# A hybrid decoder trunk on one core: the instruction order of every engine computed with another machine model of the library

## The chip, the cores and the metric

The kernel runs on one core of one Trainium2 chip. The metric is device time in microseconds of one launch; lower is better. The time before is 1925.44 us, the median of three runs.

## The reference

Two layers over a residual stream of 1024 tokens by 1024 features, all in float32. Each layer normalises the stream, multiplies it with one wide input matrix, feeds slices of the product to four mixers, gates each mixer with its own SiLU path, multiplies the joined result with an output matrix, normalises again and adds it to the stream; then a gated embedding is added.

```python
for i in range(DEPTH):
    h = rms_norm(x, g_pre[i])
    proj = h @ w_in[i]
    (q, k_cmp, v_cmp, k_sel, v_sel, k_win, v_win, nsa_g, z_a,
     u, v, z_b, glu_a, glu_b, z_c, rw, z_d) = jnp.split(proj, split_at, axis=-1)
    y_a = nsa_attention(...)
    y_b = spatial_gating(u, v, ...)
    y_c = conv_module(glu_a, glu_b, ...)
    y_d = rwkv7_time_mix(token_shift(rw, ...), ...)
    mix = concat([y_a * silu(z_a), y_b * silu(z_b), y_c * silu(z_c), y_d * silu(z_d)])
    x = x + rms_norm(mix @ w_out[i], g_post[i])
    x = x + sigmoid(x @ ple_gate[i]) * (p[i] @ ple_proj[i])
```

The attention has a compressed, a selected and a windowed branch. The RWKV mixer is a recurrence over time, which the kernel computes in chunks of 64 tokens.

## The kernel before, in words

The work is cut into two layers and, in each, two halves of 512 tokens. For each of these four parts a string of letters in ORDER gives the steps in the order in which the program writes them: H the norm, F the RWKV projections, R the small triangular solves of RWKV, r its serial chunk steps, N and A the attention, G, T and C the convolution, s the spatial gating, a to d the gate projections, O, x and g the output projection, residual and embedding gate.

Dense products are made at full precision by splitting each float32 operand into a high and a low part: `mm3` (L163 to L165) issues three matmuls of 128x128 weights by 128x512 activations for each product. The weights come in granules of 128x512: `split_w` (L149 to L159) loads one by SyncE's queue (L154), ScalarE casts its high part (L157), GpSimd subtracts to get the low part (L158). Each of the three tiles has a ring of three buffers, and these four instructions carry a priority 4000 places ahead of where they are written:

```python
with self.tc.high_priority(offset=4000):
    st = self.t([128, 512], "ws")
    for ap, w in src:
        nc.sync.dma_start(ap(st), w)
    hi = self.t([128, 512], "wh", dt=F32R)
    lo = self.t([128, 512], "wl", dt=F32R)
    nc.scalar.copy(hi[:, :cols], st[:, :cols])
    nc.gpsimd.tensor_sub(lo[:, :cols], st[:, :cols], hi[:, :cols].bitcast(F32))
```

PSUM has two banks for dense products ("mm"), two for attention scores ("s"), and one each for RWKV ("rp", "c1"), transposes ("pt") and attention sums ("pv").

Nothing in the kernel writes out an engine's queue. The program is traced in the order of ORDER and handed to the library's tile scheduler when the TileContext closes. The scheduler is a list scheduler: it steps a machine model through time; whenever the model says that an engine can take an instruction, the scheduler gives it, of those whose inputs and buffers the model says are ready, the one with the highest priority (the place in the program, moved ahead by `high_priority`). The sequence in which an engine was given its instructions becomes its queue, and on the chip each queue runs in that order: an instruction whose input is late holds all that stand behind it on its engine. SyncE's queue of DMA issues is made in the same way. So the model's durations decide the order and nothing else: the tiles, the buffers, the instructions and their dependencies come from the program.

Places that the prediction speaks of:

- `compress_out` (L846 on): on TensorE L856 (first product of the compression, on weights that a DMA brings) and L862, on ScalarE L866, on VectorE L867 (SiLU), on TensorE L870 (second product).
- `rwkv_solve` (L444 on): on VectorE a serial loop of 15 and one of 16 rounds; the second is L500 (multiply) and L502 (reduce).
- `rwkv_tri` L533 and L539, `rwkv_pair` L377, `a_block` L438 and L441.
- `rwkv_step` (L558 on), eight times in a half: TensorE L578 and L582, ScalarE L585, TensorE L589, VectorE and ScalarE L591 and L592, TensorE L602, VectorE L611, TensorE L616. Each group of matmuls waits for the other engine's result just before it, and L582 of the next step waits for L611.
- `rwkv_norm` (L620 on): GpSimd L630 (a power, 16 elements per partition), for which VectorE's L632 waits. `rstd` L243 is the same operation with 1 to 4 elements; L265 on TensorE waits for it.
- `branch` (L975 on): scores L994 and L995, exponent L1024 on ScalarE, L1029 on VectorE scales the probabilities; `attn_tile` L957 transposes them on TensorE, L960 and L961 split them, L966 and L967 multiply with the values.
- `conv_taps` L683: 240 multiply-adds of 128x512 on VectorE.

## Time and profile before

| | us |
|---|---|
| median of 3 runs | 1925.44 |
| the three runs | 1922.86, 1925.44, 1941.99 |
| the profiled execution's own time | 1919.29 |
| its span, first to last instruction | 1917.6 |
| TensorE busy in the span | 1725.0 |
| VectorE, ScalarE, GpSimd busy | 1383.7, 813.6, 612.2 |

The rows of the profile come from the one profiled execution. An engine's idle time before an instruction is put down to the engine or DMA whose result came last ("<-"). The end of a matmul is modelled, so its duration is longer than the time until the next one can start: the distance between starts is the better measure of what a matmul costs in a dense run.

### The profile page before, as it was taken

The page shows a single profiled execution, that of the slowest core. Times are in us where ns is not written, and L with a number is a line of the kernel's source. Part 1 is how long each engine was busy: PE and PEld are TensorE (multiplying, and loading weights), DVE is VectorE, ACT ScalarE, POOL GpSimd, SP SyncE. Part 2 cuts the span into 40 slices and gives each one's busy share as a digit, 9 for nine tenths or more (in the row PEclk, how much of TensorE's full clock was granted, in tenths as well). Part 3 has the DMA queues.
Part 4 walks back from the last instruction along what each step waited for, and adds up shares of the span by engine and source line. Part 5 has one row for each costly group of instructions (what it writes and reads, how often), then busy time and mean ns, then how long its engine had stood idle before and what let it go on. Part 6 is the DMA issues. An engine that isn't in the chain of part 4 may idle for free. (4 is left out here: it accounts for less than half of the span.)

```text
span 1917.6 us, 27663 instructions
## 1 busy us (share of the span) xinstructions
PE 1725.0 (90%) x9444; PEld 1296.7 (68%) x9444; DVE 1383.7 (72%) x3361; ACT 813.6 (42%) x1805; POOL 612.2 (32%) x487
## 2 busy tenths in 40 slices
PE   5797998899799999899888999989988989989998
PEld 4565776566577667666666767766666767766777
DVE  4449787887888865977578881869778789476554
ACT  4332234544223455655232343545432445545543
POOL 2223343122342333322233346322232232422253
PEclk8898999999899999999998999999998999979999
DMA  6435233123432231532253233542253223223444
GB/s 208 90 87 107 71 97 84 45 57 64 114 81 78 67 99 63 169 106 55 60 123 78 69 115 117 166 121 56 62 113 79 53 57 115 66 72 109 139 139 152
DMA packets 326148, 182.23 MB, mean 95 GB/s; under 512 B 88300, under 2 KB 299248, under 8 KB 326008
## 3 DMA queue, kind: packets, MB, share of 16 engines
q1 hardware_dynamic: 326008, 180.47, 34.7%
q8 instruction: 74, 1.21, 0.3%
q14 instruction: 66, 0.54, 0.1%
HBM read 149.98 MB, written 30.44 MB: 94 GB/s over the span
## 5 line engine op out<-in xcount | busy, mean ns | idle before, releaser
L158 POOL TENSOR_TENSOR wl<-ws,wh 128x512 fp32r<-128x512 f32 (+2 forms) x388 | 521.6, 1346 | 1160.7 <-ACT wh L157 1021.0
L163 PE MATMUL mm<-aT,wh 128*128 128x512 f32 (+1 forms) x1304 | 538.2, 416 | 16.6 <-ACT t L667 7.4
L164 PE MATMUL mm<-aT,wh 128*128 128x512 f32 (+1 forms) x1304 | 536.3, 411 | 8.3 <-DVE aT L252 8.0
L165 PE MATMUL mm<-aT,wl 128*128 128x512 f32 (+1 forms) x1304 | 535.4, 411 | 0.4 <-POOL wl L158 0.4
L157 ACT CAST wh<-ws 128x512 fp32r<-128x512 f32 (+2 forms) x388 | 236.9, 611 | 454.3 <-PE mm L164 229.4
L163 PEld LDWEIGHTS mm<-aT,wh 128*128 128x128 f32 (+1 forms) x1304 | 251.0, 193 | 71.0 <-ACT t L667 7.9
L164 PEld LDWEIGHTS mm<-aT,wh 128*128 128x128 f32 (+1 forms) x1304 | 252.1, 193 | 60.5 <-DVE aT L252 15.2
L165 PEld LDWEIGHTS mm<-aT,wl 128*128 128x128 f32 (+1 forms) x1304 | 251.6, 193 | 48.2 <-issue 2.6
L683 DVE SCALAR_TENSOR_TENSOR cv<-cv,cw,cv 128x512 f32<-128x512 f32 x240 | 213.4, 905 | 3.2
L961 DVE TENSOR_TENSOR pt<-pt,pt 128x512 fp32r<-128x512 f32 (+1 forms) x152 | 93.7, 617 | 122.2 <-ACT pt L960 120.9
L1024 ACT ACTIVATE r<-s,sma 128x512 f32<-128x512 f32 (+3 forms) x192 | 106.2, 555 | 111.2 <-DVE sma L1022 76.3
L960 ACT CAST pt<-pt 128x512 fp32r<-128x512 f32 (+1 forms) x152 | 80.3, 528 | 112.7 <-PE pt L957 112.3
L957 PE MATMUL pt<-cst,r 128*128 128x128 f32 x528 | 98.4, 282 | 21.9 <-DVE r L1029 16.9
L957 PEld LDWEIGHTS pt<-cst,r 128*128 128x128 f32 x528 | 64.2, 143 | 50.8 <-DVE r L1029 26.3
L967 PE MATMUL pv<-pt,vs 128*128 128x256 f32 x264 | 79.0, 317 | 11.8 <-DVE pt L961 10.2
L966 PE MATMUL pv<-pt,vs 128*128 128x256 f32 x264 | 84.7, 321 | 2.4 <-ACT pt L960 2.1
L994 PE MATMUL s<-kv,qs 128*128 128x512 f32 (+2 forms) x192 | 75.6, 394 | 4.9 <-ACT r L1024 4.7
L1029 DVE TENSOR_SCALAR r<-r,sma 128x640 f32<-128x640 f32 (+7 forms) x128 | 76.1, 595 | 0.8
L967 PEld LDWEIGHTS pv<-pt,vs 128*128 128x128 f32 x264 | 50.6, 192 | 35.1 <-DVE pt L961 28.3
L966 PEld LDWEIGHTS pv<-pt,vs 128*128 128x128 f32 x264 | 50.6, 192 | 32.3 <-ACT pt L960 26.7
L995 PE MATMUL s<-kv,qs 128*128 128x512 f32 (+2 forms) x192 | 65.7, 345 | 0.0
L994 PEld LDWEIGHTS s<-kv,qs 128*128 128x128 f32 x192 | 37.1, 193 | 34.5 <-ACT r L1024 27.2
(333 smaller groups left out, 2904.1 us busy)
## 6 DMA issues: line engine op xcount, KB each, us to landing
ws<-in_w_in_dram SPq DMA_DIRECT2D x232, 256.0 KB, 2.9
ws<-in_ple_gate_dram SPq DMA_DIRECT2D x64, 256.0 KB, 2.8
ws<-in_w_out_dram SPq DMA_DIRECT2D x60, 256.0 KB, 2.8
ped<-ot SPq DMA_DIRECT2D x32, 256.0 KB, 3.4
ld<-in_nsa_w_dram SPq DMA_DIRECT2D x32, 256.0 KB, 3.5
ld<-ped SPq DMA_DIRECT2D x32, 256.0 KB, 3.5
mixd<-y SPq DMA_DIRECT2D x30, 256.0 KB, 2.0
ld<-mixd SPq DMA_DIRECT2D x30, 256.0 KB, 3.0
```

Source lines behind the costliest of these rows:

```text
L157: nc.scalar.copy(hi[:, :cols], st[:, :cols])
L158: nc.gpsimd.tensor_sub(lo[:, :cols], st[:, :cols], hi[:, :cols].bitcast(F32))
L163: nc.tensor.matmul(out, lh, rh, start=first, stop=False, skip_group_check=shared)
L164: nc.tensor.matmul(out, lh, rl, start=False, stop=False, skip_group_check=shared)
L165: nc.tensor.matmul(out, ll, rh, start=False, stop=last, skip_group_check=shared)
L683: nc.vector.scalar_tensor_tensor(ac, xg[j][:, k:k + TH], cw[:, j * 31 + k:j * 31 + k + 1], ac, op0=OP.mult, op1=OP.add)
L957: nc.tensor.transpose(pt[:, o:o + 128], P[e][:, (b + x - b0) * 128:(b + x - b0) * 128 + 128], self.ident)
L961: nc.vector.tensor_sub(Tl[:, :n], pt[:, :n], Th[:, :n].bitcast(F32))
L966: nc.tensor.matmul(acc, vs, Th[:, x * 256:x * 256 + 256], start=False, stop=False)
L967: nc.tensor.matmul(acc, vs, Tl[:, x * 256:x * 256 + 256], start=False, stop=last)
L994: nc.tensor.matmul(p[:, :n], w.QS[hd][:, qs], w.KH[br, hh][:, c0 * 128:c1 * 128], start=True, stop=False)
L1024: nc.scalar.activation(P[:, o:o + wd], p[:, c:c + wd], AF.Exp, bias=ng[:, 0:1], accum_out=den[:, x:x + 1])
```

## The change

One argument of the TileContext. The scheduler now steps the library's timeline machine instead of its core machine. The timeline machine walks each instruction through its sequencer, its engine's queue, the engine and its semaphores as separate resources; the core machine is the library's default model. The traced program, its 27663 instructions, their tiles, priorities and buffer rings stay as they are; the order of each engine's queue is what comes out differently.

```diff
-    with _tile.TileContext(nc) as tc:
+    with _tile.TileContext(nc, schedule_with_timeline_sim=True) as tc:
         tile_trunk_kernel(tc, aps)
```

## Rows read from the trace of the kernel before

**Rows 1.** The page, first lines: span, and TensorE's busy time, share, instructions.

```profile
span 1917.6 us, 27663 instructions
...
PE 1725.0 (90%) x9444; PEld 1296.7 (68%) x9444; DVE 1383.7 (72%) x3361; ACT 813.6 (42%) x1805; POOL 612.2 (32%) x487
```

**Rows 2.** The waits of TensorE: total us, times, longest us.

```profile
PE pt L870 <- DVE cth L867: 17.4, 3, 8.2
PE pt L957 <- DVE r L1029: 16.9, 23, 3.5
PE pt L856 <- DMA ld<-in_nsa_w_dram: 10.9, 9, 3.3
PE rp L377 <- ACT t L374: 10.3, 1, 10.3
PE pv L967 <- DVE pt L961: 10.2, 17, 3.8
PE mm L163 <- ACT t L1054: 10.2, 1, 10.2
PE rp L533 <- DMA x<-Xd: 9.0, 4, 5.3
PE mm L163 <- ACT t L667: 7.4, 2, 6.9
PE mm L163 <- ACT ot L1063: 7.2, 3, 6.5
PE c L441 <- DVE q L459: 7.0, 4, 2.3
PE mm L265 <- POOL smc L243: 6.3, 6, 1.4
```

**Rows 3.** The timeline of TensorE in layers 0 and 1: start, duration, what [idle before].

```profile
177.88 0.43 PE L870 MATMUL pt<-cth,w 128*64 128x31 f32 x4 [8.22 <-DVE cth L867]
...
1442.17 0.43 PE L870 MATMUL pt<-cth,w 128*64 128x32 f32 x4 [8.23 <-DVE cth L867]
1442.53 0.80 PE L165 MATMUL mm<-aT,wl 128*128 128x512 f32 x1
```

**Rows 4.** The timeline of VectorE just before the second of these.

```profile
1441.25 0.61 DVE L500 TENSOR_TENSOR q<-l,q 128x248 f32<-128x248 f32 x1
1441.89 0.22 DVE L867 SCALAR_TENSOR_TENSOR cth<-cth,pt 128x64 f32<-128x64 f32 x1
```

**Rows 5.** The timeline of TensorE, 641 to 647 us.

```profile
646.03 0.30 PE L957 MATMUL pt<-cst,r 128*128 128x128 f32 x1 [3.53 <-DVE r L1029]
646.09 0.48 PE L163 MATMUL mm<-aT,wh 128*128 128x512 f32 x1
```

**Rows 6.** The timeline of VectorE at the same place.

```profile
643.62 1.25 DVE L632 TENSOR_SCALAR yt<-yt,bmv,bmr 128x64 f32<-128x64 f32 x1 [2.90 <-POOL bmr L630]
...
645.34 0.54 DVE L1029 TENSOR_SCALAR r<-r,sma 128x640 f32<-128x640 f32 x1
```

**Rows 7.** Groups of instructions: count, busy us, mean ns, idle before us.

```profile
L630 POOL TENSOR_TENSOR bmr<-bmr,mhalf 128x16 f32<-128x16 f32 x4 | 12.2, 3054 | 1.1 <-DVE bmr L629 1.0
```

**Rows 8.** Stretches: length, busy time of the five engines, granted clock, DMA share, GB/s.

```profile
1441.00:1448.00 7.00, 5.83 (x20) 4.25 (x21) 5.48 (x13) 2.13 (x7) 0.24 (x1) 0.61 0.18 16
1152.00:1176.00 24.00, 23.79 (x105) 19.32 (x105) 1.20 (x2) 9.86 (x18) 14.39 (x13) 1.00 0.45 138
```

**Rows 9.** The timeline of TensorE: the same group in two successive RWKV steps.

```profile
612.51 0.82 PE L616 MATMUL c<-l,at 64*64 64x64 f32 x8
...
620.75 0.82 PE L616 MATMUL c<-l,at 64*64 64x64 f32 x8
```

**Rows 10.** The timeline of TensorE in a dense stretch, three matmuls apart.

```profile
1160.08 0.39 PE L163 MATMUL mm<-aT,wh 128*128 128x512 f32 x1
...
1160.76 0.39 PE L163 MATMUL mm<-aT,wh 128*128 128x512 f32 x1
```

**Rows 11.** One line, the convolution taps: ns min/median/max, first and last start.

```profile
L683 DVE SCALAR_TENSOR_TENSOR cv<-cv,cw,cv x240: 681/750/1859, 179.7 to 1612.2; 128x512 f32<-128x512 f32 x120
```

## The prediction

> **What bounds the kernel now.** I read the page first: TensorE is busy 1725.0 us of a span of 1917.6 [rows 1], so it is idle 1917.6 - 1725.0 = 192.6 us. The second engine, VectorE, is busy 1383.7 us and stays under the span by 534 us. TensorE sets the time, and since the change leaves its instructions alone, what an order can give is a part of the 192.6 us and of what the clock takes. The second view is TensorE's waits [rows 2]: the reader is to see that the long entries are not dense matmuls (L163 to L165) that starve for weights. GpSimd's low part of the weights is not among the long entries. They are small matmuls of the chains (L870, L957, L967, L533, L441) that stand at the head of the queue while their input is late. The third view is the timeline at two of these places. At 1442.17 us L870 had waited 8.23 us for VectorE's L867 [rows 3], and the matmul right behind it is L165, the third of a dense product whose first two were already done: its operands were there, and it could have run in the wait, with what follows it. VectorE came late because L867 stands behind the rounds of the solve, the last but a reduce of which began at 1441.25 [rows 4]. The same wait occurs in layer 0, 8.22 us long [rows 3], and the two make most of the 17.4 us of rows 2; so it is not chance: the machine that made the order had VectorE through the solve some 8 us earlier, against TensorE, than the chip has it. The second place is of the same kind: TensorE's L957 waits 3.53 us with a dense L163 behind it [rows 5]; its input L1029 stands on VectorE behind L632, which itself waited 2.90 us for GpSimd's L630 [rows 6], a power that takes 3.05 us four times [rows 7]. A queue that knew of these 3 us would have put L1029 and what it needs ahead of L632.
>
> **What the change does to these terms.** It removes and adds no instruction, so every duration stays; what moves is the place of instructions in five queues, SyncE's DMA issues included. I take the waits of rows 2 in three classes.
>
> Waits for a result of VectorE or GpSimd whose lateness the order misjudged, with dense work behind: L870 17.4, L957 16.9, L265 6.3, together 40.6 us. The cover is there: a dense product of three matmuls starts every 0.68 us [rows 10], so 8 us of wait is 36 of them, as many as three granules hold. The ends are 0 (the new order misjudges the same) and 40.6; I take 35, since two of the three lines show their cause in the rows and the cause is one of durations, which is what a machine model has to offer.
>
> Waits on hops and DMA landings: L856 10.9, L967 10.2, L533 9.0, L441 7.0, together 37.1 us. Here the issue and the use are both in the order's hands, but the chains in question are tight, with 17 waits of L967 that average 0.6 us. Ends 0 and 37.1; I take a quarter, 9, the value nearest to the many short waits.
>
> Waits that have no other work behind them, or are of dense matmuls themselves: on L374 10.3 (L377, at the start, before other work exists), on L1054 10.2, on L667 7.4, on L1063 7.2, together 35.1 us. They wait for operands or for a PSUM bank to be emptied. Ends: 35.1 saved to 35.1 lost, as an order can relieve or deepen them; I take 0.
>
> [...]
>
> New waits: no trace shows them. The smallest long row of rows 2 that is a chain wait is L441 with 7.0, the largest L870 with 17.4; I take 7 as the price of one new place, and keep 0 and 52 (three times 17.4) as ends.
>
> VectorE's and ScalarE's own waits are not priced, as only what reaches TensorE counts; SyncE's issues are in the class of the DMA waits. Moving the weight splits is costed at nothing because the ring of three granules hides them now, as TensorE's long waits show none on them [rows 2]; if that cover went, a granule late is 4 x 0.68 = 2.7 us.
>
> One thing no order can settle in advance: a tap of the convolution takes 681 to 1859 ns for the same shape [rows 11], so either machine's clock for VectorE drifts from the chip's in these stretches. [...]
>
> Sum: 35 + 9 + 5 - 7 = 42 us. The profiled execution took 1919.3 us, so 1877. The median of the runs stands 6.1 us above it, so I forecast 1883 us for the median, 2.2% less than 1925.4.
>
> **The rivals.** First, slower: the timeline machine has a queue in front of each engine as a resource of its own, and so an instruction may be given to an engine long before it starts. If the scheduler fills such a queue with ready dense matmuls, a chain matmul that becomes ready a moment later goes behind them, for good. The place is the RWKV step: L616 follows L616 after 620.75 - 612.51 = 8.24 us [rows 9], with three groups of matmuls in turn (L589, L602, L616 with the next L582) that each answer to another engine. One granule more ahead of each is 4 x 0.68 = 2.72 us [rows 10], three times in a step and 32 steps: 261 us of longer chains, 65 in each of the four parts. TensorE does other work meanwhile, as long as there is any: the rival decides where the attention, gates and projections that the buffers admit are used up before the chain ends. If a quarter stays uncovered it costs 65 us: 1925 + 65 = 1990. For it: TensorE has gaps in the serial stretches already, so the remaining work there is thin. Against it: a queue with more dense work between hops also has fewer waits of the class of 37.1.
>
> Second, no change: the gaps are set by buffers. In the trace the cases for it are L667 and L1063, 14.6 us of PSUM banks; the chain waits of 77.7 speak against it. If filling a wait early only makes the two dense banks or the three granules run out sooner, the gain of 42 comes back as waits of the third class: 1920 to 1930. [...]
>
> Third, it does not do what it says: priorities and dependencies fix the queues so tightly that the order hardly differs; 1925.
>
> **How the numbers follow.** The forecast 0.50, the slower rival 0.30, the buffers 0.14, no new order 0.06. About 1% is what a measurement of this kernel can tell from no change, that is 1906 to 1945. So faster 0.50, same 0.20, slower 0.30. The forecast's own range is 1842 (all of 40.6 and 37.1 and the clock, 83 us) to 1906. The whole range begins lower, at 1815: a third of the 79.8 us of idle that the listed rows leave (192.6 - 77.7 - 35.1) may go with the rest, 83 + 27 = 110. It ends at 1990, the price of the slower rival; a tenth lies above it, where more than a quarter of the chain is bare, and less below the lower end.
>
> **What would show it.** Right: the two 8.2 us waits before L870 gone, the 17.4 under 4; L957's 16.9 under 8; TensorE idle at 150 us or less with the same busy time; L632 on VectorE no longer with L1029 behind it in its wait. The slower rival: the distance of L616 to L616 well over 8.24 us, and TensorE's idle time in stretches with little dense work. The buffers: the idle time moves from chain lines to L163 waiting for ScalarE or VectorE. The forecast is wrong if TensorE's idle time grows, or if its idle time falls and the busy time grows as much, by more switches between small and dense matmuls or a lower clock.

## The result, and the profile after

The kernel after takes 2106.53 us in the median (2097.53 to 2117.51), the kernel before 1933.72 us beside it: a ratio of 1.092 [1.088, 1.097]. The change makes it 9% slower; the forecast was 2.2% faster. The profiled execution of after took 2117.51 us; it stands 198 us above that of before. The medians differ by 173 us: after's profiled execution is the slowest of its four, and before's is faster than the four that the ratio goes by.

The page of after: span, busy times, then four of the rows with 40 equal slices of the span.

```profile
span 2115.8 us, 27584 instructions
...
PE 1866.7 (88%) x9444; PEld 1445.2 (68%) x9444; DVE 1364.4 (64%) x3361; ACT 810.1 (38%) x1805; POOL 632.4 (30%) x487
...
PE   4899789889969999899979999899997999989878
...
PEclk8999775579979887999969897999997958779879
DMA  7344320012434200442332331352433301045133
```

The same two last rows of before:

```profile
PEclk8898999999899999999998999999998999979999
DMA  6435233123432231532253233542253223223444
```

TensorE has the same 9444 matmuls, and it is busy for 1866.7 us in place of 1725.0 [rows 1]; it is idle for 2115.8 - 1866.7 = 249.1 us in place of 192.6. The page counts 79 instructions fewer than before's 27663: all of them are semaphore instructions of the queues; the five engines' own counts are the same. The larger part is in the busy time, and the row of the clock says why: in before it is at 8 or 9 in all slices but one; in after it is at 5 in the 7th, 8th and 33rd, and there the DMA row is at 0: hardly any weights move (16, 26 and 16 GB/s, where the mean is 86), and not one dense matmul starts in these three slices. The mean granted clock is 0.855 against 0.954. The trace records two levels of it, 0.5 and 1.0 of full speed, and none between (after is at 0.50 from 289 to 301 us, and at 1.00 from 117 to 196), so that is 2 x (1 - 0.855) x 2115.8 = 614 us at the lower one, and 176 us in before.

I split the 198 us from the starts of TensorE's matmuls: the median distance to the next start at the full clock, for each line and shape, is streaming; what goes over it while the half clock is granted, up to as much again, is put to the clock; the rest are gaps. Between the first and the last matmul before has 1455 + 59 + 389 us and after 1454 + 193 + 454. So some 134 of the 198 us are the clock, 65 gaps, and nothing is streaming; with before's medians for both kernels it is 142, 51 and 6. This is bookkeeping, and its share of the clock is an upper one, since a wait that falls into the half clock is counted as clock up to one median. Nor has a microsecond at the half clock one price: tm_pe4 below has 94 us more of it than before, and takes the same time.

TensorE's waits in after (total us, times, longest):

```profile
PE pv L966 <- ACT pt L960: 18.4, 32, 1.3
PE s L994 <- ACT r L1024: 18.1, 20, 3.6
PE mm L163 <- ACT ot L1063: 17.8, 13, 3.2
PE pt L957 <- DVE r L1029: 16.4, 15, 3.8
PE pv L967 <- DVE pt L961: 14.4, 20, 3.3
PE mm L163 <- DVE t L733: 12.8, 6, 7.0
PE rp L533 <- DMA x<-Xd: 12.5, 8, 5.4
PE mm L163 <- DVE y L648: 11.1, 8, 3.7
PE s L163 <- ACT aT L251: 10.0, 2, 7.9
...
PE mm L265 <- POOL smc L243: 2.1, 1, 2.1
PE pt L856 <- DMA ld<-in_nsa_w_dram: 2.0, 3, 1.3
```

L870, the longest row of [rows 2], is gone from the list; L441 too; L856 fell from 10.9 to 2.0, L265 from 6.3 to 2.1. L957 stayed (16.9 to 16.4), L967 and L533 grew. So of the 77.7 us that the prediction wanted to shrink 38 went and 8 came back. New ones stand in the attention: L966 had 2.1 us in before, L994 4.7. And the dense L163 waits longer for ScalarE and VectorE: 69.8 us over all such rows, in place of 35.0. That is 35 of the 56.5 us by which the idle time grew; whether operands or banks are late there isn't shown.

Where the time comes from is seen in one part (layer 0, first half), cut at the end of the RWKV front end (L422), the first round of the solve, and the first L533. Only the matmuls into the tile mm are counted here, nearly all of them dense products: start and end, length, busy us (count), granted clock, DMA share, GB/s. Before:

```profile
108.00:144.00 36.00, 24.81 (x94) 1.00 0.40 94
144.00:192.00 48.00, 31.16 (x120) 0.86 0.51 109
192.00:301.00 109.00, 65.12 (x285) 0.97 0.32 88
```

After:

```profile
117.00:196.00 79.00, 66.63 (x262) 1.00 0.46 113
196.00:289.00 93.00, 60.63 (x289) 0.84 0.36 85
289.00:429.00 140.00, 1.70 (x8) 0.56 0.07 22
```

From the front end to the solve, 262 dense matmuls run in place of 94, and the stretch takes 79 us in place of 36. Under the triangular solves and the chunk steps before has 285 (253 of L163 to L165, and 32 of L773); after has 8, all of L259, the next part's norm, and not one dense product. The steps run with some attention beside them, at a clock of 0.56, in 140 us in place of 109.

The other three parts aren't copies of this one. From their first L533 to their last L616, before:

```profile
524.00:636.00 112.00, 64.06 (x278) 0.95 0.29 78
1017.00:1127.00 110.00, 65.09 (x280) 0.96 0.27 75
1457.00:1563.00 106.00, 54.82 (x224) 0.98 0.23 59
```

After:

```profile
686.00:850.00 164.00, 51.88 (x195) 0.80 0.15 47
1098.00:1334.00 236.00, 139.59 (x610) 0.90 0.30 84
1663.00:1839.00 176.00, 50.67 (x188) 0.73 0.14 43
```

In the second and fourth the front end is filled as in the first (271 and 255 dense matmuls up to the solve, before 78 and 92), and the steps have less dense work than before and a lower clock. In the third the front end is as in before (77, before 96), and the steps are overfull: 576 dense matmuls in place of 247. At the last L616 of the four parts after is 128, 214, 207 and 277 us behind before, and 198 at the end: the first two parts, layer 0, make the larger share, the last one adds to it, and its tail gives some back.

How this came about is in TensorE's queue. Just behind L422 before has (one dense matmul at the place of the first dots, two at that of the second):

```profile
112.82 0.49 PE L438 MATMUL rp<-ab,ab 64*128 64x128 f32 x3
...
113.67 0.71 PE L438 MATMUL c<-ab,ab 64*128 64x128 f32 x4
114.31 0.44 PE L519 MATMUL rp<-cst,ab 128*128 128x128 f32 x2
...
115.15 0.33 PE L441 MATMUL c<-ab,ab 64*64 64x64 f32 x2
115.41 0.71 PE L438 MATMUL rp<-ab,ab 64*128 64x128 f32 x4
```

and after, with six and then fourteen dense matmuls between two hops, that is between one group of the chain's matmuls and the next (L163, L164 and L165 in turn at the place of the dots):

```profile
126.85 0.71 PE L438 MATMUL c<-ab,ab 64*128 64x128 f32 x4
127.48 0.50 PE L165 MATMUL mm<-aT,wl 128*128 128x512 f32 x1
...
128.98 0.38 PE L519 MATMUL rp<-cst,ab 128*128 128x128 f32 x2
129.12 0.48 PE L165 MATMUL mm<-aT,wl 128*128 128x512 f32 x1
...
132.50 0.71 PE L438 MATMUL c<-ab,ab 64*128 64x128 f32 x4
```

In these rows a hop every 0.3 to 0.9 us became a hop every 2 to 4 us. No idle time shows it: from L422 to the solve TensorE has one gap of 1.1 us in 79, and the full clock. It shows later, as work that is missing under the steps.

### The profile page after: what moved, and what is told of

Read it like the earlier page. It is cut to its first block, busy times and chain, and to the rows that moved or that the text cites. A ratio compares the mean times of both kernels' runs of the same rounds, so it can differ in the third digit from the quotient of the medians.

```text
span 2115.8 us, 27584 instructions
## 1 busy us (share of the span) xinstructions
PE 1866.7 (88%) x9444; PEld 1445.2 (68%) x9444; DVE 1364.4 (64%) x3361; ACT 810.1 (38%) x1805; POOL 632.4 (30%) x487
## 5 line engine op out<-in xcount | busy, mean ns | idle before, releaser
L158 POOL TENSOR_TENSOR wl<-ws,wh 128x512 fp32r<-128x512 f32 (+2 forms) x388 | 543.1, 1404 | 1048.0 <-ACT wh L157 975.2
L163 PE MATMUL mm<-aT,wh 128*128 128x512 f32 (+1 forms) x1304 | 543.1, 418 | 23.8 <-DVE t L733 12.8
L164 PE MATMUL mm<-aT,wh 128*128 128x512 f32 (+1 forms) x1304 | 533.8, 410 | 6.9 <-DVE aT L252 6.9
L165 PE MATMUL mm<-aT,wl 128*128 128x512 f32 (+1 forms) x1304 | 532.3, 408 | 0.5 <-POOL wl L158 0.5
L163 PEld LDWEIGHTS mm<-aT,wh 128*128 128x128 f32 (+1 forms) x1304 | 255.6, 196 | 94.5 <-DVE t L733 11.6
L164 PEld LDWEIGHTS mm<-aT,wh 128*128 128x128 f32 (+1 forms) x1304 | 255.3, 196 | 66.1 <-DVE aT L252 8.8
L165 PEld LDWEIGHTS mm<-aT,wl 128*128 128x128 f32 (+1 forms) x1304 | 254.0, 195 | 61.7 <-issue 4.9
L683 DVE SCALAR_TENSOR_TENSOR cv<-cv,cw,cv 128x512 f32<-128x512 f32 x240 | 220.7, 939 | 1.5
L957 PE MATMUL pt<-cst,r 128*128 128x128 f32 x528 | 118.2, 331 | 17.0 <-DVE r L1029 16.4
L966 PE MATMUL pv<-pt,vs 128*128 128x256 f32 x264 | 99.6, 381 | 18.8 <-ACT pt L960 18.4
L967 PE MATMUL pv<-pt,vs 128*128 128x256 f32 x264 | 95.8, 374 | 15.3 <-DVE pt L961 14.4
L994 PE MATMUL s<-kv,qs 128*128 128x512 f32 (+2 forms) x192 | 88.0, 459 | 18.8 <-ACT r L1024 18.1
L598 POOL TENSOR_TENSOR q<-SB,gc 128x256 f32<-128x256 f32 x28 | 19.0, 677 | 274.0 <-DVE SB L611 231.5
L957 PEld LDWEIGHTS pt<-cst,r 128*128 128x128 f32 x528 | 77.2, 166 | 28.4 <-DVE r L1029 15.7
L966 PEld LDWEIGHTS pv<-pt,vs 128*128 128x128 f32 x264 | 62.0, 235 | 39.2 <-ACT pt L960 29.2
L967 PEld LDWEIGHTS pv<-pt,vs 128*128 128x128 f32 x264 | 63.0, 239 | 30.6 <-DVE pt L961 23.5
L995 PE MATMUL s<-kv,qs 128*128 128x512 f32 (+2 forms) x192 | 74.7, 394 | 0.0
```

What stands on the lines that cost most here:

```text
L163: nc.tensor.matmul(out, lh, rh, start=first, stop=False, skip_group_check=shared)
L164: nc.tensor.matmul(out, lh, rl, start=False, stop=False, skip_group_check=shared)
L165: nc.tensor.matmul(out, ll, rh, start=False, stop=last, skip_group_check=shared)
L683: nc.vector.scalar_tensor_tensor(ac, xg[j][:, k:k + TH], cw[:, j * 31 + k:j * 31 + k + 1], ac, op0=OP.mult, op1=OP.add)
L957: nc.tensor.transpose(pt[:, o:o + 128], P[e][:, (b + x - b0) * 128:(b + x - b0) * 128 + 128], self.ident)
L966: nc.tensor.matmul(acc, vs, Th[:, x * 256:x * 256 + 256], start=False, stop=False)
```

## The experiments

Every ratio is to the kernel before on the same chip, with its 95% interval. "TM" is the timeline machine of the change, "core" the library's default. Two counts of TensorE's queue, taken from its order and not from a time, help to read the runs: **bare**, the matmuls other than L163 to L165 that stand in unbroken stretches of 60 or more; and **lumps**, the dense matmuls (L163 to L165, 4608 in all) in unbroken runs of 12 or more. The time at the half clock is worked out as above, from each run's span and mean clock, with the two levels of before and after taken for all.

| run | ratio | bare | lumps | us at half clock |
|---|---|---|---|---|
| before (core) | 1 | 444 | 2047 | 176 |
| after (TM, the library's own depths of the modelled queues) | 1.092 | 2256 | 3827 | 614 |
| tm_pe8 | 1.020 | 769 | 2171 | 309 |
| tm_pe4 | 0.999 | 455 | 2061 | 270 |
| tm_pe2 | 1.008 | 339 | 2071 | 284 |
| tm_all4 | 0.999 | 432 | 2047 | 250 |
| tm_queue_pe1 | 1.384 | 757 | 3505 | 1154 |
| tm_queue_all1 | 1.347 | 682 | 3322 | 1033 |
| tm_taps_late | 1.096 | 2088 | 3588 | 605 |
| tm_gates_held | 1.112 | 1817 | 3620 | 597 |
| tm_gates_spread | 1.132 | 1935 | 3552 | 627 |
| tm_both_spread | 1.100 | 1864 | 3443 | 628 |
| tm_hops_free | 1.091 | 2109 | 3880 | 551 |
| tm_chain_free | 1.087 | 1971 | 3627 | 564 |
| core_taps_first | 1.067 | 697 | 2384 | 409 |
| core_gates_first | 1.052 | 439 | 2445 | 371 |
| tm_pe_as_before | 1.070 | 444 | 2047 | 345 |
| core_pe_as_after | 1.176 | 2256 | 3827 | 777 |
| before_silu | 0.997 | 444 | 2047 | 197 |
| before_fill | 1.001 | 444 | 2259 | 221 |

**First theory: the taps of the convolution.** In after 60 of a part's taps stand ahead of or inside the solve's rounds on VectorE (in parts 0, 1 and 3 of 0 to 3), in before behind them (but for two in the third part). An order edge (it fixes the order of two instructions of a queue and adds no wait) puts them back, all else left to the machine; on the core machine the reverse is done in the program's order.

```diff
# after
+            self.tc.add_manual_dep(first.ins, self.solved.ins.name, NoSync)   # first tap behind the solve
# before
-ORDER = ("iXeHFBRNrGabscdnAAATCy",
+ORDER = ("iXeHFBGtRNrabscdnAAATCy",
...
```

> The changed kernel with one thing undone: in each of the four parts the first tap of the convolution is placed on VectorE behind the last instruction of the RWKV solve of that part (an order edge alone, no wait). Theory A (the timeline machine lets instructions be given to an engine far ahead of their start, so that the taps, of low priority, stand before the solve on VectorE in three of four parts and the serial RWKV chain begins some 60 taps late): the three parts get back up to 60 x 0.92 = 55 us each, so about 100 us of the 190, ratio to the kernel before 1.03 to 1.06. Theory B (the taps are a symptom, and the loss lies in TensorE's own order, dense matmuls used up early): ratio stays 1.08 or above. Theory C (any other order of this program costs as much): 1.08 or above too.

> The kernel before, on the core machine, with the convolution's input and its 60 taps written ahead of the solve in the three parts in which the changed kernel has them there (parts 0, 1 and 3); every other step as it was. Theory A: the solve starts some 55 us later in three parts, and what of this is bare shows: 60 to 165 us, ratio 1.03 to 1.08. Theory B (the taps' place is a symptom): under 1.02, because TensorE has other work in those 55 us.

Measured: 1.096 [1.092, 1.100] for taking them back, 1.067 [1.062, 1.071] for putting them first on the core machine. The second shows that this place of the taps, and of the convolution's input with them, is enough to cost 7% in an otherwise good order; the first, that in after it isn't what costs: the solve's first round (L478) still starts at 188 us (after 196, before 144). The theory falls as a cause of this change.

**The modelled queue, 1 deep.** The timeline machine may give an engine instructions ahead of their start, as many as a depth allows that the library sets for each modelled queue; after has the library's own depths. The first run sets TensorE's to 1, the second all five.

```diff
+    _spec.ENG_ISSUE_QUEUE_DEPTH = {**_spec.ENG_ISSUE_QUEUE_DEPTH, _e.PE: 1}
     with _tile.TileContext(nc, schedule_with_timeline_sim=True) as tc:
```

> The changed kernel, with the timeline machine told that TensorE's issue queue holds one instruction instead of its own number (the other engines' queues as they are); only the order comes out differently. Theory A: dense matmuls are no longer committed ahead of chain matmuls, the RWKV front and the solve come in time, the taps fall behind the solve by themselves; ratio to the kernel before 0.99 to 1.03. A theory by which the machine's durations make the order bad, whatever the queue: 1.07 or above. Theory C (the program was fitted to the core machine's order and any other loses): 1.02 to 1.06.

> As the last, with all five issue queues of the timeline machine one deep. Theory A: like the last or a little better, 0.98 to 1.02, since VectorE's and ScalarE's queues can't be filled ahead of the chain either. Durations as the cause: 1.07 or above. Theory C: 1.02 to 1.06.

Measured: 1.384 [1.374, 1.394] and 1.347 [1.340, 1.353], far outside what theories A and C foresaw, and inside the open range (1.07 or above) of the theory of the machine's durations. In the first part the chain came as early as in before (solve at 140 us), and yet more was lost than in after, with 3505 dense matmuls in lumps. I read it first as evidence against the depth. That was too quick, as the next runs show; why a depth of 1 makes so poor an order stays open.

**Is it TensorE's queue, and is it the depth?** The program is scheduled twice: TensorE's sequence under one machine is held, by an order edge from each instruction to the next, while the other machine orders the four other queues; and TensorE's modelled queue is set to a depth of 4 (tm_pe4) and of 8 (tm_pe8), in place of the library's own, with all else as in after.

```diff
+    other = [i.name for i in build(timeline=False).all_instructions() if i.engine == PE]
+    for p, n in zip(other, other[1:]):
+        tc.add_manual_dep(ins[n], p, NoSync)
```

> The timeline machine makes all queues, but TensorE's queue is held by order edges to the sequence that it has in the kernel before; VectorE, ScalarE, GpSimd and SyncE are ordered by the timeline machine around it. Theory D (the loss comes from TensorE's queue alone: the gate projections and the spatial gating, some 240 to 336 dense matmuls a part, stand ahead of the serial RWKV chain, and the chain then runs without dense work and at the half clock): the loss goes, ratio to before 0.98 to 1.02, VectorE free to be a little better or worse, TensorE's granted clock back at 0.94 to 0.96 against 0.855 in after. Rival E (the prices of VectorE, ScalarE and the DMA issues in the timeline machine give poor orders of those queues): most of the loss stays, ratio 1.05 to 1.10, clock under 0.90.

> The reverse: the core machine makes all queues, but TensorE's queue is held by order edges to the sequence that it has in the kernel after. Theory D: the loss comes with that queue, ratio to before 1.07 to 1.12, granted clock 0.84 to 0.88. Rival E: ratio 0.99 to 1.03, clock over 0.93.

> [...] The gate projections that stand ahead of the first triangular solve fall from 336, 333, 0, 336 dense matmuls in the four parts to 58, 29, 22, 48 (kernel before: 0, 88, 111, 72), and from the first solve to the last chunk step there are 278, 319, 386, 319 dense matmuls (before 252, 243, 246, 216; after 0, 195, 576, 188). Theory D with the deep modelled queue as its cause: most of the loss goes, ratio 0.99 to 1.03, clock 0.92 to 0.96. Rival E: ratio 1.05 to 1.10. A depth of 1 gave 1.384, which D puts down to a modelled TensorE that can't load weights beside its matmuls at that depth; if 4 is above 1.10 too, the depth is not the cause as D says it.

> As with 4, but 8 deep: gate projections ahead of the first solve 165, 168, 20, 80 dense matmuls, between it and the last chunk step 171, 282, 436, 343. Theory D: between the run with 4 and after, ratio 1.02 to 1.07, clock 0.88 to 0.94. Rival E: 1.05 to 1.10, no order with the run at 4.

Measured: at depth 4 the loss is gone, 0.999 [0.996, 1.002], at 8 it is 1.020 [1.013, 1.026]. The second lies at the lower edge of its range (1.02 to 1.07). With 1.092 at the library's own depth, which is larger, the time follows the depth from 4 upward, and so do the bare matmuls and the half clock. The part shown above, at depth 4 (same cuts):

```profile
106.00:143.00 37.00, 28.62 (x107) 1.00 0.38 91
143.00:201.00 58.00, 43.03 (x167) 0.94 0.53 116
201.00:349.00 148.00, 72.73 (x318) 0.85 0.26 69
```

The hops to the solve take 37 us again, and 318 matmuls into mm are left for the steps. The steps take 148 us, longer than in after (140), and the time is that of before: longer steps by themselves aren't the loss. Theory D missed both mixed runs: TensorE's queue of before among queues of the timeline machine takes 1.070 [1.064, 1.076], that of after among queues of the core machine 1.176 [1.169, 1.182]. The first is inside the range of the rival E, which blamed the other queues; but with the machine's own queue for TensorE at depth 4 the same machine loses nothing, so its durations don't force the loss. A queue isn't good by itself; that the five are made for one another, and that granules, banks and results come at other times when four of them are exchanged, is the likely reason and wasn't traced. So TensorE's queue alone isn't shown to be the whole loss; the depth that makes it is.

Two more depths: 2 for TensorE's queue (tm_pe2), and at most 4 for all five (tm_all4).

> The timeline machine with the modelled queue in front of TensorE 2 deep. Gate projections ahead of the first solve 52, 16, 28, 48 dense matmuls, close to the 58, 29, 22, 48 at depth 4. If only the place of the filler counts (D1, D2), 0.99 to 1.02 as at depth 4 (0.999). If a depth of 1 lost 38 per cent because a shallow modelled TensorE is slowed by its own queue, a part of that shows at 2: 1.03 to 1.15.

> [...] TensorE's counts are nearly those of depth 4 on TensorE alone. If TensorE's depth is the whole cause: 0.99 to 1.01, no different from 0.999. If the run-ahead of the other queues cost something that the deep TensorE queue hid: 0.96 to 0.99, a kernel that beats both.

Measured: 1.008 [1.005, 1.011] and 0.999 [0.997, 1.001]. Of the depths tried 4 is the best, and beside it the depth of the other engines' queues (4 or the library's own) makes no difference that these runs can tell. Beside a TensorE queue 1 deep it did: 1.347 against 1.384.

**Which way does the depth do it?** D: the gate projections and the spatial gating (240 to 336 dense matmuls a part) are used up ahead of the chain. F: a run of dense matmuls goes ahead of each hop. Five runs of order edges on after, and one change of the program's order on the core machine.

```diff
+        if self.gates:                        # dense products of a, b, s, c, d
+            with self.tc.issue_after(self.marks[0]):      # held: first triangular solve
+            with self.tc.issue_after(self.marks[self.held]):   # spread: k-th behind the k-th mark
```

> After, with the modelled queues as they are, and every dense product of the gate projections and the spatial gating behind the first triangular solve of its part on TensorE by an order edge. Dense matmuls counted on TensorE's queue up to the first solve: 432, 1152, 2304, 3456 in the four parts (before 428, 1152, 2322, 3456; after 768, 1485, 2256, 3796); but behind it they come in lumps: 235, 192, 216 and 216 of them stand between the solve and the end of the first chunk step, and none in some of the last steps. Theory D1 (what matters is that this filler stands ahead of the chain's solve): ratio to before 1.00 to 1.04. Theory D2 (what matters is that it stands in lumps between the hops, as a deep modelled queue lets a whole run of ready dense matmuls go ahead of each hop): most of the loss stays, 1.05 to 1.09.

> The same products held by order edges one by one: the k-th dense product (24 matmuls) of these steps behind the k-th mark of the chain (the first triangular solve, then the last matmul of each chunk step). Dense matmuls up to the solve as in the run before it; then 24 to 80 a step. D1: 1.00 to 1.04, like the held run. D2: better than the held run by 3 per cent or more, ratio 0.99 to 1.03. A third theory, E (TensorE's queue is harmed in many other places too, and the gates are only a part): 1.03 to 1.07 in both runs.

Measured: 1.112 [1.109, 1.115] and 1.132 [1.126, 1.137], both worse than after. All three theories miss. The edges have a price of their own: in the held run the DMAs fall to 5 or 6 GB/s in three of the page's slices, probably because products that wait for a mark hold the three granules. And they empty a stretch that was full. From the solve's first round to the first L533 the matmuls into mm were 120 in before and 289 in after in the first part (shown above); in the held run there is none, and the clock is half:

```profile
186.00:252.00 66.00, 0.00 (x0) 0.50 0.10 12
```

The same holds in the spread run and in the next one, in three of the four parts. So these runs don't test D alone. The next run holds the weight loads too, and the taps:

```diff
# core_gates_first, on before
-ORDER = ("iXeHFBRNrGabscdnAAATCy",
+ORDER = ("iXeHFBabsRNrGcdnAAATCy",
...
# tm_both_spread, on the spread run
+                    self.tc.add_manual_dep(d.ins, self.after.name, NoSync)   # weight load behind the mark
```

> After, with the convolution's taps behind the triangular solve on VectorE, and the products of the gate projections and the spatial gating behind the chain's marks one by one, their weight loads too (so that the three granules aren't held by products that wait for a mark). Between the hops of the chain ahead of the solve stand the same runs of dense matmuls as in after. Theory D with both of its parts: ratio to before 1.00 to 1.04. Theory F: 1.05 or more, the solve's first round still some 30 us later after the part's front end than in the kernel before.

> The core machine, and only the place of the gate projections a and b and of the spatial gating in the program is changed: they are written ahead of the triangular solves. Dense matmuls on TensorE's queue up to the first solve: 659, 1392, 2533, 3696 (before 428, 1152, 2322, 3456); few stand between the hops of the chain ahead of it, as before. Theory D (this filler used up ahead of the chain is the harm, whatever the machine): ratio to before 1.05 to 1.10, granted clock under 0.92. Theory F (the harm is a run of dense matmuls ahead of every hop, a chain matmul that becomes ready goes behind them; the place of the gates is its consequence): 1.00 to 1.05, since the hops stay short.

Measured: 1.100 [1.096, 1.103], the solve still at 183 us; and 1.052 [1.049, 1.056] on the core machine. So D alone can cost 5% (its forecast began at 1.05, F's ended there), and undoing D and the taps by these edges does not help after. Then the hops:

```diff
# tm_hops_free: dense products of G, N, a, b, s, c, d and their weight loads
+        self.after = self.ablk                # last L441 ahead of the solve
# tm_chain_free: that for G and N; gates spread, taps behind the solve
```

> After, with every dense product of the convolution's inputs, of the attention's inputs, of the gate projections and of the spatial gating (and the loads of their weights) behind the last matmul of the chain's L441 ahead of the solve, by order edges. Between the hops from L422 to the solve stand then no such matmuls (after: 2 to 18 a hop, about 10), and up to the first triangular solve 398, 1142, 2160, 3446 dense matmuls (before 428, 1152, 2322, 3456); behind it the gate projections still come in lumps of 200 and more in the first chunk step. Theory F1 (the run of dense matmuls ahead of each hop before the solve is what makes the chain late, and the chain's lateness is the loss): ratio to before 0.99 to 1.04, the solve's first round back at some 145 us instead of 196. Theory F2 (the same at every hop of the whole program, the chunk steps and the attention too): the solve comes early, but 1.05 to 1.10 remains.

> After with all three held: no dense matmuls of these steps between the hops ahead of the solve, the gate projections one by one behind the first triangular solve and the chunk steps, the taps behind the solve. F1: 0.98 to 1.03. F2: better than the run before it, since the chunk steps have their dense matmuls evenly too, but the attention keeps its lumps: 1.03 to 1.08.

Measured: 1.091 [1.087, 1.096] and 1.087 [1.081, 1.093]. The solve does start early, at 142 and 143 us as in before, and the loss stays. F1 as it was put falls: an early solve doesn't bring the time back. But these edges too go past before: they leave 17 to 34 dense matmuls between L422 and the solve where before has 78 to 96, and in the first part that stretch is granted 0.52 in place of 1.00. F2 has the first ratio inside its 1.05 to 1.10 and missed the second, for which it foresaw 1.03 to 1.08; the two runs can't be told apart. The page of tm_hops_free shows the dips of the clock again, at other places than in after:

```profile
PEclk9979986698978989989699899999898997898579
```

The table has the reading that fits these runs: in all six versions of after with edges 1817 to 2109 matmuls stay in bare stretches, and 3443 to 3880 dense ones in lumps. Taking the lumps from one place puts them at another, and no edge run puts the dense work back where before has it. What the depth changes, and none of these edits does, is the grain of the whole queue. That this grain is the cause is argued from the counts and not shown by itself; the depth is shown. Nor do the counts order all rows: core_gates_first loses 5% with 439 bare, as few as before, and 2445 in lumps, where tm_pe8 loses 2% with 769 and 2171; tm_queue_pe1 loses 38% with 757 and 3505; and the two mixed runs lose with the counts of queues that they took over. How much each place carries (chain, steps, attention) stays open.

**Are the waits that the forecast counted on worth their time?** The five queues of before are held to their own sequence, by edges. In one run only L867 moves ahead of six rounds of the solve, in two parts; in the other 283 dense matmuls on TensorE move ahead of the matmul that waits in front of them, in 78 places.

```diff
+    dve.insert(near[-6], dve.pop(k))          # before_silu: L867 ahead of the last six L500
+    pe[k:k] = [at[n] for n in dense]          # before_fill: dense matmuls into the wait
```

> The kernel before with all five queues held to their sequence; only in the first and the last part VectorE's L867 is moved ahead of the last six rounds of the solve. This is the first term of the prediction's sum, had alone: its two waits of 8.2 us before L870 should shrink to about 2 us each, the dense work behind them moving up: 10 to 13 us, ratio 0.993 to 0.995. If the time doesn't follow (ratio 0.997 to 1.003), such a wait is given back later in the part.

> The kernel before with all five queues held to their sequence; only on TensorE 283 dense matmuls are moved ahead of the matmul that waits in front of them, in 78 places where the trace of the kernel before shows a wait of over 0.35 us and their operands and their bank as ready by then. Nothing else is moved, and no more dense matmuls than fit in the wait, so no hop of the chain is made later. If the idle time that the prediction counted on can be had by order alone: up to 283 x 0.227 = 64 us, ratio 0.967 to 0.985. If moved dense work only leaves a hole where it was (buffers and weights set the pace): 0.995 to 1.005.

Measured: 0.9974 [0.9953, 0.9994] and 1.0007 [0.9990, 1.0023]. before_silu gains 5 us (1 to 9 by the interval), less than the 10 to 13 expected and just inside the range that it gave for a wait that comes back. Two of its waits:

```profile
PE pt L870 <- DVE cth L867: 8.0, 3, 3.1
PE pt L885 <- ACT vct L883: 7.4, 2, 3.7
```

L870 has 8.0 us left of 17.4, so the edit removed 9.4 and not 16; and 7.4 us of a wait at L885, a few matmuls further on in the same chain, are new (0.4 in before). before_fill gains nothing of up to 64 us, though waits did move. Its page's line and TensorE's waits:

```profile
PE 1754.7 (91%) x9444; PEld 1314.2 (68%) x9444; DVE 1387.0 (72%) x3361; ACT 812.2 (42%) x1805; POOL 612.0 (32%) x487
...
PE rp L533 <- DMA x<-Xd: 12.9, 4, 3.6
PE pt L957 <- DVE r L1029: 12.4, 15, 3.6
...
PE pt L870 <- DVE cth L867: 8.2, 3, 4.4
PE s L994 <- ACT r L1024: 8.1, 19, 1.2
```

L870 has 8.2 us left of 17.4 and L957 12.4 of 16.9, but L533 went from 9.0 to 12.9 and L994 from 4.7 to 8.1; TensorE's idle time fell by 12 us only (1935.1 - 1754.7 = 180.4), and its busy time rose by 30 us, at a clock of 0.943. How much of the return is the clock and how much new waits stays open, because the two profiled executions stand at different places: before's is 11.6 us under the median of before in this comparison (1930.92), before_fill's 3.9 us over its own.

before_silu is the one kernel that is faster than before and after by more than its interval: by a quarter of a per cent, and barely.

## Why the prediction was wrong

**What bounds the kernel** held: TensorE, with chain matmuls waiting ahead of dense ones. **The late results**, 40.6 us, were to shrink, and L870 (17.4) and L265 (6.3 to 2.1) did; L957 did not (16.9 to 16.4). Of the hop class L856 and L441 went, L967 and L533 grew. So the forecast's first sign, L870 under 4, came true in a kernel that is 9% slower: a sign that a wait is gone, and none that the time is. Its sign of being wrong came true too: TensorE's idle time grew.

Three steps failed.

First, "the cover is there". The sum took a wait that is filled as time gained. before_silu and before_fill measure that step by itself: some 5 us for 9.4 us of removed wait, most of which came back at L885, and nothing for up to 64. Moving dense work adds none; filled into one wait, it can be missing later. The rival of the buffers, which had 0.14, is not contradicted by this: order alone got nothing from those waits in before_fill. That buffers are the reason isn't shown.

Second, "New waits: I take 7", and 0 for the waits of dense matmuls. The waits of L163 alone grew by 35 us, as much as the worse end that the prediction kept for that class. And the larger harm was no new wait at the place where it is done. Between L422 and the solve TensorE has almost no gap in after; the price was 43 us of a longer chain in the first part, and 253 dense matmuls that are missing under the steps. Of the slower rival this is the mechanism, word for word (ready dense matmuls are given ahead, and a chain matmul that becomes ready goes behind them), at a place that it hadn't named. The place that it had named, the steps, is hit so in the third part alone, with its 576 dense matmuls; in the first the steps are longer with none among them, near the half clock (0.54 from 321 to 429 us). From the first L616 to the last it is 107, 123, 160 and 126 us in the four parts, in place of 75, 76, 74 and 75: 215 us together, near the 261 that the rival worked out, but only in one part for its reason. What the prediction set against it, that such a queue has fewer waits, held for some rows of the list and has no bearing on the time. It had 0.30 and should have had the larger share: the prediction knew that the machine has a queue in front of each engine, and a depth is a number that can be looked up.

Third, the clock, 5 us of gain in the sum, and "every duration stays". No run shows those 5 us: [rows 8] have a low clock behind one long wait, but before_silu, with 9.4 us less of these waits, has a mean clock of 0.949 against 0.954 in before, and after, where they are gone, 0.855. The instructions stayed, their durations did not: TensorE's busy time rose by 142 us. The sum has the clock as a gain alone. The rival's 1990 us had no clock in it; some 134 of the 198 us are the clock. The rival's end of the range failed for that. That its 65 us equal the 65 us of gaps is luck: it had them as a quarter of longer steps left uncovered. By its busy time alone such a chain doesn't look bad: TensorE is busy 126.64 us of 140 in the last of the three stretches of after, all matmuls counted, and this at 0.56.

## What to carry to other kernels

A scheduler that may hand instructions to a queue long before they start filled it here with whatever was ready, and what is ready is the work that could have waited; the serial chain then stands behind it. Before trusting such an order, count on the queue itself how many dense matmuls lie between two hops of the chain and how long the stretches without any are: that costs no run, and here it separates 1.00 from 1.09 among the orders that one machine made at depths of 2, 4, 8 and the library's own. It doesn't rank every order of the table. Read a removed wait as gained only when you can say where the work that fills it comes from and what lies under its old place.

## What the runs showed of the hardware that was not expected

The share of the clock in a loss that is only one of order: by the split above the half clock adds some 59 us to the same 9444 matmuls in before and some 193 us in after. The small matmuls of a chunk step at the half clock (0.50 from 331.5 to 333.2 us in after), the same group as in [rows 9] (0.82 us there, at the full clock, 1.00 from 612 to 622 us):

```profile
331.72 1.30 PE L616 MATMUL c<-l,at 64*64 64x64 f32 x8
```

From 292.0 to 331.7 us, ahead of this row, TensorE was busy 33.90 us of 39.70 without one dense product, and was granted 0.63; in before, with 253 of them spread over the same steps, the stretch of 109 us was granted 0.97.
